# First weights split around the token gather, the last expert's down projection in plain fp32, and two pieces of issue order moved in a one-core transformer layer

## The chip, the cores and the metric

The kernel runs on 1 core of one Trainium2 chip. The metric is device time in microseconds (us) of one execution; lower is better. A run's time lies a little above the span of its trace, which goes from the first to the last instruction.

## The reference

One backbone layer over 1024 latent tokens and 256 context tokens, width 1024: a mixer (latent attention in parallel with a bidirectional mLSTM, merged and projected), then a mixture of 16 SwiGLU experts in which every expert chooses its 128 tokens, then a final RMSNorm. Everything is float32. The part that the change is about, cut:

```python
aff = softmax(x @ w_router)                       # (1024, 16)
g, idx = top_k(aff.T, 128)                        # each expert takes 128 tokens
xs = x[idx]                                       # gathered tokens, per expert
a = xs @ w_e_gate[e]; u = xs @ w_e_up[e]          # 1024 x 1024 each
y = (silu(a) * u) @ w_e_down[e] * g[e]            # 1024 x 1024
out = rmsnorm(x + g2 * scatter_add(idx, y), final_norm)
```

Attention: `p = softmax(q k^T * scale)`, `o = p v`, 8 heads, 1024 queries by 1280 keys.

## The kernel before

Nearly every matmul is done in three fp32r products. A float32 operand is cut into `hi` (ScalarE, a cast to fp32r, an ACT CAST in the rows) and `lo = raw - hi` (VectorE, a DVE TENSOR_TENSOR); the product is hi·hi + hi·lo + lo·hi. The class `Weights` (L769 on) brings the expert weights in blocks of 128x2048 (1 MB each, 12 per expert: 8 for the gate and up projection, 4 for the down projection, index `j`), on the queue of SyncE (SP), 14 raw buffers ahead. `Weights.split` (L862) makes `hi` (L879) and `lo` (L880) of a block; there are three buffers of each (`N_HI`). Instructions are ordered by a planner: it takes those that it thinks ready, by the order in which the program names them; `tc.high_priority()` puts a stretch ahead, and `tc.issue_after(x)` keeps what is in it behind `x` on `x`'s engine.

**Routing and the first tokens.** `Merge.rest` (L1056) ends with the last tile's router and the sort that finds each expert's threshold; it calls `W.split(1)` (L1167), so block 0 is cut there. `moe` (L1178) builds a mask from the threshold, calls `W.split(2)` behind the count of the mask (L1234), sums the mask by matmuls into `pre`, and makes `taken` (L1245), which stands behind the low part of block 1, and `slot` (L1247). `mark(e)` (L1250) writes a one-hot matrix of the expert's tokens: on VectorE for expert 0 (L1256), by eight GpSimd (POOL) instructions for the others (L1254). `pick(e)` (L1259) turns it into token numbers by eight small matmuls and gathers the tokens with an indirect DMA that GpSimd issues (L1278). Behind the matmuls of `pick(0)` eleven matmuls with no use for their result keep TensorE busy. `turn_x(e, q)` (L1292) transposes half of the gathered tokens on TensorE (L1299), scales and shifts them out of PSUM (L1307; for expert 0 half of them on VectorE, L1305) and cuts them into `xh`, `xl` (L1183, L1184).

**The expert loop** (L1341). For expert `e`, two half passes of four blocks each (`products`, L1311) fill `pa` and `pu`; `act` (L1327) makes silu(pa)·pu; `turn` (L1283) transposes that and cuts it into `hd`, high by ScalarE (L1289) and low by VectorE (L1290). Then four blocks of the down projection fill `py`. Between them stand, in this order: `turn` of the second half behind block 0, `pick(e + 2)` and `turn_x(e + 1, 0)` behind block 1, `turn_x(e + 1, 1)` behind block 2. All of them write transposes or sums into one PSUM name, `tr`, which has two buffers. At the end VectorE scales `py` into `y` (L1371), and GpSimd adds it into `acc_d` in HBM by an indirect DMA (L1372).

**The last expert** (L1377 to L1440). Its own 128 rows are gathered back from `acc_d` (L1378), and all 1024 rows are loaded from `acc_d` (L1388) as eight tiles. The last four weight blocks are cut like the others and kept whole (L1406), the down projection runs as 48 fp32r matmuls, column half after column half (L1408 to L1416), and only then come the eight tiles' norm: squares on ScalarE (L1397), an inverse root of about a dozen small VectorE instructions (`rstd_dve`, L143), and the scaling by VectorE (L1400) with a store for each tile. The expert's own rows are put together in `z` (L1421, L1422), normed with them (L1423) and written last, by an indirect DMA that waits for all eight stores (L1436).

**Attention** (L1443 on) works in 32 groups of 256 queries. `scores(g)` ends with the running maximum halved (L1554); behind it stands `low(g - 1, 0)`, the low part of one block of the previous group's exponentials (L1619). `peak(g)` transposes the maxima (L1563) and reduces them to `mq` (L1566), with `low(g - 1, 1)` behind it; `peak2(g)` spreads `mq` by two more transposes (L1573).

Of the kernel before, what the change touches and what calls it, by code (L numbers as in the profile page):

```python
# [23 lines left out]
F32 = mybir.dt.float32  # L24
# [9 lines left out]
P = 128  # L34
# [734 lines left out]
class Weights:  # L769
# [92 lines left out]
    def split(self, upto, engine=None):  # L862
        while self.cut < min(upto, 12 * NE):
# [3 lines left out]
            if not 12 * NE - 4 <= j < 12 * NE - 2:  # L867
                hi, lo = self.halves()
            else:
                hi, lo = [self.buffer(2 * j - 12 * NE + 6 + x, F32R) for x in range(2)]  # L870
            self.parts[j] = hi, lo
# [10 lines left out]
            if self.cut == upto:  # L882
                return done
# [90 lines left out]
class Merge:  # L974
# [81 lines left out]
    def rest(self, aff, thr, pool):  # L1056
# [110 lines left out]
        W.split(1)  # L1167
# [10 lines left out]
def moe(tc, A, out, aff, thr, W, h2_d, acc_d, ident, bcols, rstd, dump):  # L1178
    nc = tc.nc
    V, S, G, TE = nc.vector, nc.scalar, nc.gpsimd, nc.tensor  # L1180

    def split(hi, lo, raw):
        S.copy(hi, raw)  # L1183
        V.tensor_sub(lo, raw, hi)  # L1184
# [4 lines left out]
    with ExitStack() as st:  # L1189
# [43 lines left out]
        with tc.issue_after(counted.ins):  # L1233
            done = W.split(2)  # L1234
# [24 lines left out]
        def pick(e):  # L1259
# [23 lines left out]
        def turn(src, hi, lo, q):  # L1283
# [5 lines left out]
            S.copy(hi[:, 4 * q:4 * q + 4, :], t3)  # L1289
            V.tensor_sub(lo[:, 4 * q:4 * q + 4, :], t3, hi[:, 4 * q:4 * q + 4, :])  # L1290

        def turn_x(e, q):  # L1292
# [4 lines left out]
            for c in range(4):  # L1297
                k = 4 * q + c
                TE.transpose(tr[:, c * P:(c + 1) * P], xg[e][:, k * P:(k + 1) * P], ident)  # L1299
# [9 lines left out]
            split(hi, lo, t)  # L1309
# [16 lines left out]

        def act(pa, pu):  # L1327
# [6 lines left out]
        picked, got, W.after = pick(0)  # L1334
        for q in range(2):
            turn_x(0, q)
# [4 lines left out]
        for e in range(NE):  # L1341
            j = 12 * e
            hd = []
            hs = []
# [12 lines left out]
            if e + 1 < NE:  # L1357
                for q in range(4):
# [18 lines left out]
            rows = p7.tile([P, D], F32, name="xg", bufs=2)  # L1377
            G.indirect_dma_start(out=rows, out_offset=None, in_=acc_d,  # L1378
                                 in_offset=bass.IndirectOffsetOnAxis(ap=idx[e][:, :1], axis=0))
            fn = p7.tile([P, D], F32, name="y", bufs=1)  # L1380
            nc.sync.dma_start(fn, rows_bcast(A["final_norm"], D))
            junk = W.narrow().bitcast(BF16)
            xs, stores = [], []
            for m in range(4):
                x = W.buffer(12 * NE + 2 + m)
                for a in range(2):
                    i = 2 * m + a
                    nc.sync.dma_start(x[:, a], acc_d[i * P:(i + 1) * P])  # L1388
                xs += [x[:, 0], x[:, 1]]
            ss = p7.tile([P, 10], F32, name="fss")  # L1390
# [680 lines left out]
```

## Time and profile before

| | |
|---|---|
| time, median of 3 runs | 2005.15 us (2004.23 to 2007.27) |
| the profiled execution: its own time, its span | 2006.65 us, 2004.9 us |
| mean granted TensorE clock | 0.983 |
| TensorE (PE) busy | 1906.5 us, 95% of the span |
| VectorE (DVE), ScalarE (ACT), GpSimd (POOL) busy | 1397.4 us, 1060.5 us, 554.3 us |
| moved by DMA | 384.77 MB, mean 192 GB/s |

Times in rows are microseconds from the span's start, or the length of an instruction. A row of the timeline has the start, the length, the engine, the line, the operation, what it writes and reads, and in brackets the idle time of the engine before it with what ended it. PE rows of length 0.39 overlap: matmuls are pipelined, so their pace is read from start to start. Plain fp32 matmuls appear as two records each, fp32r ones as one.

### The profile page before, as it was taken

Reading aid. Unit: us, or ns where it says so; the run is one execution under the profiler, and the core shown is the slowest. Engines: PE = TensorE matmul, PEld = TensorE weight load, DVE = VectorE, ACT = ScalarE, POOL = GpSimd, SP = SyncE. Lnnn points to the kernel's source line nnn. Section 1 sums busy time; section 2 is a strip of 40 time slices with the busy share of each in tenths; the row PEclk is TensorE's granted clock in tenths of the full one; section 3 lists DMA queues with packets and bytes.
Section 4 is the critical chain, followed back from the end, with each engine's and each line's share of the span. In section 5 each row is a group of like instructions: output and inputs, shape, how many; then the busy total and the mean of one; then the engine's idle time right before and its main releaser. Section 6 shows DMA issues by size and latency. Waiting matters only on the chain. (4 is left out here: it accounts for less than half of the span.)

```text
span 2004.9 us, 28234 instructions
## 1 busy us (share of the span) xinstructions
PE 1906.5 (95%) x10454; PEld 1607.3 (80%) x10454; DVE 1397.4 (70%) x2492; ACT 1060.5 (53%) x1611; POOL 554.3 (28%) x491
## 2 busy tenths in 40 slices
PE   7999999999999999899999999996999999999994
PEld 3898888888877878789999898884787878878873
DVE  6454555112367788676777768667899999999897
ACT  5554421212336686534334344332778778787774
POOL 0000000000034022165544445001445646455400
PEclk9999999999999999999999999997999999999997
DMA  7153376223069060311311111547799999999984
GB/s 307 55 148 99 117 241 217 88 84 110 32 234 327 6 218 30 93 56 56 102 51 51 49 48 44 210 153 274 270 372 387 382 380 388 383 385 381 377 285 185
DMA packets 156746, 384.77 MB, mean 192 GB/s; under 512 B 10160, under 2 KB 94720, under 8 KB 138432
## 3 DMA queue, kind: packets, MB, share of 16 engines
q1 hardware_dynamic: 141552, 328.68, 45.6%
q0 software_dynamic: 12752, 45.90, 7.4%
q10 hardware_dynamic: 2304, 8.39, 1.0%
q8 instruction: 82, 1.34, 0.3%
q14 instruction: 56, 0.46, 0.1%
HBM read 326.00 MB, written 56.93 MB: 191 GB/s over the span
## 5 line engine op out<-in xcount | busy, mean ns | idle before, releaser
L85 PE MATMUL mm<-hT,whi 128*128 128x512 f32 (+1 forms) x1392 | 415.0, 381 | 2.6 <-DVE hT L304 2.3
L85 PEld LDWEIGHTS mm<-hT,whi 128*128 128x128 f32 x1392 | 255.1, 189 | 51.9 <-DVE hT L304 2.4
L85 PE MATMUL mm<-hT,wlo 128*128 128x512 f32 (+1 forms) x696 | 262.9, 378 | 0.3 <-DVE wlo L89 0.3
L880 DVE TENSOR_TENSOR lo<-raw_l,hi 128x2048 fp32r<-128x2048 f32 x92 | 210.8, 2298 | 21.9 <-ACT hi L879 19.6
L1254 POOL TENSOR_SCALAR g<-iota,slot 128x128 bf16<-128x128 f32 x120 | 206.5, 1733 | 0.0
L879 ACT CAST hi<-raw_l 128x2048 fp32r<-128x2048 f32 x92 | 176.1, 1916 | 34.6 <-PE pu L1187 25.8
L1187 PE MATMUL py<-hi,hd 128*128 128x512 f32 x496 | 168.3, 401 | 0.0
L85 PEld LDWEIGHTS mm<-hT,wlo 128*128 128x128 f32 x696 | 131.3, 189 | 24.6 <-DVE wlo L89 0.7
L89 DVE TENSOR_TENSOR wlo<-wraw,whi 128x1024 fp32r<-128x1024 f32 x38 | 46.5, 1223 | 140.9 <-ACT whi L88 140.9
L880 DVE TENSOR_TENSOR lo<-xca,hi 128x2048 fp32r<-128x2048 f32 x54 | 123.6, 2297 | 17.5 <-ACT hi L879 16.5
L1610 POOL TENSOR_TENSOR es<-es,e 128x512 f32<-128x512 f32 x96 | 124.8, 1300 | 7.0
L1604 ACT ACTIVATE e<-s 128x512 f32<-128x512 f32 x160 | 94.4, 611 | 48.7 <-PE s L1450 48.7
L879 ACT CAST hi<-xca 128x2048 fp32r<-128x2048 f32 x54 | 102.9, 1907 | 25.5 <-PE pu L1187 19.7
L1610 POOL TENSOR_TENSOR es<-e 128x512 f32<-128x512 f32 x32 | 41.7, 1302 | 263.7 <-ACT e L1604 263.7
L88 ACT CAST whi<-wraw 128x1024 fp32r<-128x1024 f32 x38 | 40.0, 1051 | 128.2 <-PE mm L85 124.4
L1550 DVE TENSOR_TENSOR mx<-mx,s 128x512 f32<-128x512 f32 x128 | 87.8, 686 | 27.2 <-PE s L1450 24.6
L1278 POOL DMA_INDIRECT xg<-h_d,idx x16 | 35.8, 2235 | 255.9 <-PE tr L1299 238.2
L1187 PEld LDWEIGHTS py<-hi,hd 128*128 128x128 f32 x496 | 92.1, 188 | 17.7 <-ACT hd L1289 0.2
L1187 PE MATMUL pa<-lo,xh 128*128 128x512 f32 x256 | 100.3, 392 | 3.4 <-DVE lo L880 3.4
L1187 PE MATMUL pa<-hi,xh 128*128 128x512 f32 x256 | 101.4, 396 | 0.3 <-ACT xh L1183 0.3
L1578 ACT CAST qm<-sm 64x256 fp32r<-64x256 f32 x32 | 11.8, 367 | 167.8 <-PE sm L1573 167.8
L1187 PE MATMUL pu<-hi,xl 128*128 128x512 f32 x256 | 100.3, 392 | 0.0
(499 smaller groups left out, 4998.0 us busy)
## 6 DMA issues: line engine op xcount, KB each, us to landing
raw_l<-in_wgu SPq DMA_DIRECT2D x60, 1024.0 KB
xca<-in_wgu SPq DMA_DIRECT2D x37, 1024.0 KB
raw_l<-in_wd SPq DMA_DIRECT2D x32, 1024.0 KB
ha<-in_wgu SPq DMA_DIRECT2D x20, 1024.0 KB
wraw<-in_win SPq DMA_DIRECT2D x38, 512.0 KB
xca<-in_wd SPq DMA_DIRECT2D x19, 1024.0 KB
wt<-in_wmod_b SPq DMA_DIRECT2D x32, 512.0 KB
vk_d<-vk SPq DMA_DIRECT2D x16, 640.0 KB
```

The costliest lines, as they stand in the source:

```text
L85: return TE.matmul(o, l, r, start=start, stop=stop, skip_group_check=True)
L88: S.copy(hi, raw)
L89: V.tensor_sub(lo, raw, hi)
L879: self.nc.scalar.copy(h, w)
L880: done = (engine or self.nc.vector).tensor_sub(l, w, h)
L1187: return TE.matmul(o, l, r, start=start, stop=stop, skip_group_check=True)
L1254: G.tensor_scalar(oh[:, o, :], iota, slot[:, o, e:e + 1], None, op0=ALU.is_equal)
L1278: got = G.indirect_dma_start(out=xg[e], out_offset=None, in_=h2_d, in_offset=bass.IndirectOffsetOnAxis(ap=idx[e][:, :1], axis=0))
L1550: V.tensor_max(new if p > 1 else new.rearrange("p (a b) -> p a b", a=2), old, ps if p > 1 else ps.rearrange("p (a b) -> p a b", a=2))
L1578: S.copy(qm[64:], row[64:])
L1604: S.activation(E[p], ps, AF.Exp)
L1610: G.tensor_add(s, E[0] if p == 1 else s, E[p])
```

## The change

The diff, cut to its core:

```diff
 class Weights:
-    def split(self, upto, engine=None):
-        while self.cut < min(upto, 12 * NE):
+    def split(self, upto, later=None):
+        while self.cut < min(upto, 12 * NE - 4):
...
             for h, l, w in views:
                 self.nc.scalar.copy(h, w)
-                done = (engine or self.nc.vector).tensor_sub(l, w, h)
+                if later is None:
+                    self.nc.vector.tensor_sub(l, w, h)
+                else:
+                    later.append(lambda h=h, l=l, w=w: self.nc.vector.tensor_sub(l, w, h))
 class Merge, rest:
-        W.split(1)
+        W.lows = []
+        W.split(1, W.lows)
 def moe:
         with tc.issue_after(counted.ins):
-            done = W.split(2)
+            W.split(N_HI, W.lows)
...
-        with tc.issue_after(done.ins):
-            V.scalar_tensor_tensor(taken, pre, 1.0, mk, op0=ALU.add, op1=ALU.mult)
+        V.scalar_tensor_tensor(taken, pre, 1.0, mk, op0=ALU.add, op1=ALU.mult)
...
+        def warm(after, n):
+            with tc.issue_after(after.ins):
+                ps = ps7.tile([P, 512], F32, name="pu", bufs=2)
+                for x in range(n):
+                    mm(ps, W.parts[0][0][:, 0, :P], W.parts[0][0][:, 0, :512], True, True)
   pick:
             if e == 0:
-                with tc.issue_after(done.ins):
-                    ps = ps7.tile([P, 512], F32, name="pu", bufs=2)
-                    for x in range(11):
-                        mm(ps, W.parts[0][0][:, 0, :P], W.parts[0][0][:, 0, :512], True, True)
+                warm(done, 16)
   turn:
             S.copy(hi[:, 4 * q:4 * q + 4, :], t3)
+            if hi.dtype == F32:
+                return
   turn_x:
+            if e == 0 and q == 1:
+                warm(turned, 7)
...
         mark(0)
         picked, got, W.after = pick(0)
+        with tc.issue_after(picked.ins):
+            for f in W.lows[:2]:
+                f()
         for q in range(2):
-            turn_x(0, q)
+            done = turn_x(0, q)
+        with tc.issue_after(done.ins):
+            W.lows[2]()
...
         for e in range(NE):
+            if e == NE - 1:
+                others()
...
-                        t = W.wide_hi(F32R)
+                        t = W.wide_hi(F32R if e + 1 < NE else F32)
...
+                    if e == NE - 1 and hf == 1 and q == 2:
+                        squares(0, 2)
...
             if e + 1 < NE:
+                turn_x(e + 1, 0)
                 for q in range(4):
                     products(j + 8 + q, py, hd, q == 0, q == 3)
                     if q == 0:
                         turn(hs[1], *hd, 1)
-                    if q == 1 and e + 2 < NE:
+                    if q == 1:
+                        turn_x(e + 1, 1)
+                    if q == 2 and e + 2 < NE:
                         pick(e + 2)
-                    if q in (1, 2):
-                        turn_x(e + 1, q - 1)
...
-            W.split(12 * NE)
+            turn(hs[1], *hd, 1)
+            squares(2, 8)
+            scale(0, 2)
+            scale(2, 5)
+            scale(5, 8)
             for o in range(2):
                 for k in range(8):
-                    mm(py[o], hd[0][:, k, :], wh, k == 0, False)
-                    mm(py[o], hd[0][:, k, :], wl, False, False)
-                    mm(py[o], hd[1][:, k, :], wh, False, k == 7)
+                    mm(py[o], hd[0][:, k, :], w[:, k % 2, c], k == 0, k == 7)
+                with tc.high_priority():
+                    V.scalar_tensor_tensor(z[:, c], py[o], gat[e], g2row[:, c], op0=ALU.mult, op1=ALU.mult)
+                    V.tensor_add(z[:, c], z[:, c], rows[0][:, c])
+                    S.activation(junk[:, :512], z[:, c], AF.Square, accum_out=zs[:, o:o + 1])
+            with tc.high_priority():
+                V.tensor_add(zs[:, 0:1], zs[:, 0:1], zs[:, 1:2])
+                rstd(p7, zs[:, 2:3], zs[:, 0:1], D)
+                V.scalar_tensor_tensor(z, z, zs[:, 2:3], fn[0], op0=ALU.mult, op1=ALU.mult)
+                own = G.indirect_dma_start(out=out, out_offset=bass.IndirectOffsetOnAxis(ap=idx[e][:, :1], axis=0),
+                                           in_=z, in_offset=None)
 attention:
             MX[g] = pk.tile([P, 256], F32, name="mm", bufs=2)
-            halved = V.tensor_max(MX[g], mx[:, :256], mx[:, 256:])
-            with tc.issue_after(halved.ins):
-                low(g - 1, 0)
+            V.tensor_max(MX[g], mx[:, :256], mx[:, 256:])
...
             with tc.issue_after(found.ins):
-                low(g - 1, PARTS[1])
+                for p in PARTS[:2]:
+                    low(g - 1, p)
```

In the last expert's new loop `w` is the raw float32 block. `others()` is new and holds what stood at the head of the last expert's tail: the gather of its own rows, the load of the final norm's weights and the eight loads from `acc_d`, now into the raw buffers of blocks that are four places earlier in the rotation. `squares(a, b)` squares tiles a to b; `scale(a, b)` makes their inverse roots at once, scales them and stores each; `zs` holds the sums of `z` alone.

## Rows read from the trace of the kernel before

**Rows 1.** The page, busy time of each engine over the span

```profile
PE 1906.5 (95%) x10454; PEld 1607.3 (80%) x10454; DVE 1397.4 (70%) x2492; ACT 1060.5 (53%) x1611; POOL 554.3 (28%) x491
```

**Rows 2.** Who waited for whom, TensorE: us in total, times, longest

```profile
PE tr L1299 <- DVE hd L1290: 6.7, 13, 0.5
...
PE sm L1573 <- DVE mq L1566: 3.9, 21, 0.5
...
PE pa L1187 <- DVE lo L880: 3.4, 2, 1.7
```

**Rows 3.** Timeline from the last expert's loads to the end: start, length, engine, line

```profile
1951.55 1.91 SPq L1388 DMA_DIRECT2D raw_l<-acc_d  x4
...
1966.66 4.02 PE L1187 MATMUL py<-raw_l,hd 128*128 128x512 f32 x17
...
1978.09 0.39 PE L1187 MATMUL py<-hi,hd 128*128 128x512 f32 x1
...
1979.56 0.69 DVE L1422 TENSOR_TENSOR xg<-xg 128x512 f32<-128x512 f32 x1
...
1988.88 0.16 DVE L162 TENSOR_SCALAR rv<-fss 128x5 f32<-128x5 f32 x1
...
1991.08 4.87 DVE L1400 SCALAR_TENSOR_TENSOR ha<-ha,frs,y 128x1024 f32<-128x1024 f32 x4
...
1999.88 0.99 POOL L1436 DMA_INDIRECT out_dram<-xg,idx  x1 [47.16 <-DMA out_dram<-ha]
```

**Rows 4.** Timeline of TensorE in the mLSTM, plain fp32 matmuls of 512 columns

```profile
642.72 1.88 PE L1732 MATMUL mm<-xca,fold 128*128 128x512 f32 x4
644.44 1.99 PE L1732 MATMUL st<-qT,xca 128*128 128x128 f32 x16
```

**Rows 5.** Timeline at an expert boundary (experts 13 and 14), ScalarE

```profile
1897.08 1.91 ACT L879 CAST hi<-raw_l 128x2048 fp32r<-128x2048 f32 x1
1900.10 1.51 ACT L1307 ACTIVATE g<-tr,bcols 128x128 f32<-128x128 f32 x4 [1.11 <-PE tr L1299]
...
1903.28 0.64 ACT L1183 CAST xh<-g 128x512 fp32r<-128x512 f32 x1
```

**Rows 6.** Timeline of the routing, VectorE and TensorE

```profile
1382.85 2.27 DVE L880 TENSOR_TENSOR lo<-ha,hi 128x2048 fp32r<-128x2048 f32 x1
1382.94 0.37 PE L950 MATMUL so<-sc,ident 64*16 64x64 f32 x2 [5.14 <-DVE sc L944]
...
1390.52 0.27 PE L1187 MATMUL tr<-above,cst 128*128 128x128 bf16 x1
1391.88 0.41 DVE L1245 SCALAR_TENSOR_TENSOR g<-tr,mk 128x256 f32<-128x256 f32 x1
1392.21 2.28 DVE L880 TENSOR_TENSOR lo<-raw_e,hi 128x2048 fp32r<-128x2048 f32 x1
1394.41 0.28 DVE L1247 SCALAR_TENSOR_TENSOR slot<-g 128x128 f32<-128x128 f32 x1
```

**Rows 7.** Timeline: first gather, tokens' transposes; a later gather and low part

```profile
1397.63 1.07 POOL L1278 DMA_INDIRECT xg<-h_d,idx  x1 [17.49 <-DVE gt L1275]
...
1402.20 1.06 PE L1299 MATMUL tr<-ident,xg 128*128 128x128 f32 x8 [1.39 <-DMA xg<-h_d,idx]
...
1438.07 2.29 DVE L880 TENSOR_TENSOR lo<-raw_l,hi 128x2048 fp32r<-128x2048 f32 x1
...
1438.79 2.39 POOL L1278 DMA_INDIRECT xg<-h_d,idx  x1 [29.02 <-PE tr L1299]
```

**Rows 8.** One line's instructions, L1254: ns min/median/max, first and last start

```profile
L1254 POOL TENSOR_SCALAR g<-iota,slot x120: 590/704/4514, 1398.8 to 1881.0; 128x128 bf16<-128x128 f32 x120
```

**Rows 9.** Busy time by stretch: length, PE, PEld, DVE, ACT, POOL, granted clock, DMA

```profile
1408.00:1410.00 2.00, 2.00 (x6) 1.59 (x5) 0.00 (x0) 0.00 (x0) 1.61 (x3) 0.50 0.04 8
```

**Rows 10.** Timeline of one attention group, VectorE

```profile
1101.68 1.22 DVE L1619 TENSOR_TENSOR tl<-e,th 128x512 fp32r<-128x512 f32 x1
...
1102.83 0.41 DVE L1566 TENSOR_REDUCE mq<-sm 128x2 f32<-128x256 f32 x1
```

More of the change, by code (lines that the diff above doesn't have):

```diff
@@ L866, in split @@
             raw = self.raw[j]
[L867 to L871, printed above, removed]
+            hi, lo = self.parts[j] = self.halves()
             if j == ONCE[1]:
@@ L1308, in turn_x @@
             hi, lo = [x[:, 4 * q:4 * q + 4, :].rearrange("p a b -> p (a b)") for x in xsT[e]]
-            split(hi, lo, t)
+            S.copy(hi, t)
+            return V.tensor_sub(lo, t, hi)
         def products(j, ps, l, start, stop):
@@ L1325, in products, with others, squares, scale @@
                     mm(ps[o], ll, wh[:, slice(o * 512, o * 512 + 512)], False, stop and c == 1)
+        rows, fn, xs, stores = [], [], [], []
+        def others():
+            rows.append(p7.tile([P, D], F32, name="xg", bufs=2))
+            G.indirect_dma_start(out=rows[0], out_offset=None, in_=acc_d,
+                                 in_offset=bass.IndirectOffsetOnAxis(ap=idx[NE - 1][:, :1], axis=0))
+            fn.append(p7.tile([P, D], F32, name="y", bufs=1))
+            nc.sync.dma_start(fn[0], rows_bcast(A["final_norm"], D))
+            for m in range(4):
+                x = W.buffer(12 * NE - 2 + m)
+                for a in range(2):
+                    i = 2 * m + a
+                    nc.sync.dma_start(x[:, a], acc_d[i * P:(i + 1) * P])
+                xs.extend([x[:, 0], x[:, 1]])
+        def squares(a, b):
+            for i in range(a, b):
+                S.activation(junk, xs[i], AF.Square, accum_out=ss[:, i:i + 1])
+        def scale(a, b):
+            rstd(p7, rs[:, a:b], ss[:, a:b], D)
+            for i in range(a, b):
+                V.scalar_tensor_tensor(xs[i], xs[i], rs[:, i:i + 1], fn[0], op0=ALU.mult, op1=ALU.mult)
+                stores.append(nc.sync.dma_start(out[i * P:(i + 1) * P], xs[i]))
         def act(pa, pu):
@@ L1343, in moe @@
             hd = []
+            if e == NE - 1:
+                others()
+                junk = W.narrow().bitcast(BF16)
+                ss, rs, zs = [p7.tile([P, 8], F32, name=x) for x in ("fss", "frs", "fzs")]
             hs = []
@@ L1374, in moe @@
                 continue
[L1377 to L1390, printed above, removed]
-            rs = p7.tile([P, 10], F32, name="frs")
-            def alike(t, x):
-                return t if len(x.shape) == 2 else t.rearrange("p (c d) -> p c d", d=256)
-            def squares(k, x):
-                S.activation(alike(junk, x), x, AF.Square, accum_out=ss[:, k:k + 1])
-            def scale(k, x):
-                return V.scalar_tensor_tensor(x, x, rs[:, k:k + 1], alike(fn, x), op0=ALU.mult, op1=ALU.mult)
-            def write(i):
-                scale(i, xs[i])
-                stores.append(nc.sync.dma_start(out[i * P:(i + 1) * P], xs[i]))
-            W.split(12 * NE)
+            turn(hs[1], *hd, 1)
[3 more added lines that the diff above has]
+            scale(5, 8)
             z = p7.tile([P, D], F32, name="xg", bufs=2)
@@ L1410, in moe @@
                 for k in range(8):
-                    wh, wl = [w[:, k % 2, c] for w in W.parts[j + 8 + k // 2]]
-                    mm(py[o], hd[0][:, k, :], wh, k == 0, False)
-                    mm(py[o], hd[0][:, k, :], wl, False, False)
-                    mm(py[o], hd[1][:, k, :], wh, False, k == 7)
-                    if o == 0 and k == 1:
-                        turn(hs[1], *hd, 1)
-            squares(0, xs[0])
-            squares(1, xs[1])
-            for o in range(2):
-                c = slice(o * 512, o * 512 + 512)
-                V.scalar_tensor_tensor(z[:, c], py[o], gat[e], g2row[:, c], op0=ALU.mult, op1=ALU.mult)
-                V.tensor_add(z[:, c], z[:, c], rows[:, c])
@@ L1423, in moe @@
-            S.activation(junk, z, AF.Square, accum_out=ss[:, 8:9])
-            rstd(p7, rs[:, 0:2], ss[:, 0:2], D)
-            for i in range(2, 8):
-                squares(i, xs[i])
-            write(0)
-            write(1)
-            rstd(p7, rs[:, 2:4], ss[:, 2:4], D)
-            write(2)
-            write(3)
-            rstd(p7, rs[:, 4:9], ss[:, 4:9], D)
-            for i in (4, 5, 6, 7):
-                write(i)
-            scale(8, z)
-            own = G.indirect_dma_start(out=out, out_offset=bass.IndirectOffsetOnAxis(ap=idx[e][:, :1], axis=0),
-                                       in_=z, in_offset=None)
+                    w = W.raw[j + 8 + k // 2]
@@ new lines, in moe @@
+                    if len(w.shape) == 4:
+                        mm(py[o].rearrange("p (c d) -> p c d", d=256), hd[0][:, k, :], w[:, k % 2, 2 * o:2 * o + 2, :],
+                           k == 0, k == 7)
+                    else:
+                        mm(py[o], hd[0][:, k, :], w[:, k % 2, c], k == 0, k == 7)
[3 more added lines that the diff above has]
+                    S.activation(junk[:, :512], z[:, c], AF.Square, accum_out=zs[:, o:o + 1])
```

7 lines of the change are left out of this document (1 added, 6 removed).

## Prediction

> **What bounds the kernel now.** The page comes first: TensorE is busy for 95% of the span [rows 1], so a change gains only where TensorE stands still or has nothing left. Second, the waits of TensorE, added up by who ended them [rows 2]. Three of them belong to this change: 6.7 us before the transposes of gathered tokens (13 times 0.5), 3.9 us before the transposes of `mq`, and 3.4 us before the low part of a weight block (2 times 1.7). Third, the timeline of the end [rows 3]: the last down projection starts at 1966.66, its last matmul ends at 1978.09 + 0.39 = 1978.5, and the span ends at 2004.9. TensorE does nothing for the last 26.4 us; VectorE norms eight other tiles one after another there. Fourth, the routing [rows 6] and the first gather [rows 7], where TensorE also waits for VectorE.
>
> All sums are made against the profiled execution, 2006.65 us, of which 2004.9 are the span; the median of the runs is 1.5 us less.
>
> **1. The tail.** Call 1966.66 zero; the end now is at 38.2. *Added on TensorE:* a plain fp32 matmul of 512 columns takes 0.86 (two of them between 642.72 and 644.44 [rows 4]). Sixteen take 13.8. The fp32r ones come at 0.227 (17 within 4.02, the last 0.39 of it its own length [rows 3]); the 48 removed took 10.9. So TensorE pays 2.9. With about 0.5 for the four transposes of `hs[1]` (eight take 1.06 [rows 7]) its end moves from 11.8 to 14.3; only the first half of `hd` is needed for the first matmuls, which covers the silu, product and transposes of the second. *Removed:* the last four cuts, 1.91 of ScalarE [rows 5] and 2.3 of VectorE each [rows 6], and the norm of the others behind the matmuls. *Moved:* eight scalings (4.87 for four) and three inverse roots (2.2 each, 1988.88 to 1991.08) are 16.3 of VectorE [rows 3]. VectorE is free of cuts some 2.5 before zero, and the first tiles are loaded by then: the loads start at 1951.55, 15 before zero, when expert 14's rows are in HBM; naming them earlier cannot start them earlier. On SP's queue they stand behind all weight loads, already issued, and only the stores stand behind them. So the others are done near 14 to 15.5, their stores 3.9 later (1995.95, the last scaling's end, to 1999.88 [rows 3]), under the chain of `z`. *That chain,* from 14.3: hand-over 0.3, two steps of 0.69 [rows 3], a half row's square 0.64 (as long as the 128x512 cast [rows 5]) with 0.2 to read the sum, nine small steps of 0.2 (eleven in 2.2), scaling 1.22, 1.2 to GpSimd (an estimate between nothing and the 3.9 above), and 5.0 from the write's issue to the end (1999.88 to 2004.9): 26.1. I add 0.6 for half a scaling that VectorE may be in. **38.2 - 26.7 = 11.5 gained.** Bounds: 13.5 if every hand-over is free, 8 if two or three scalings fall behind `z`.
>
> **2. Expert boundaries.** `turn_x(e + 1, 0)` no longer follows `pick` and the turn of `hs[1]` on the two `tr` buffers: between two uses of one buffer there are now two blocks of twelve matmuls, 24 x 0.227 = 5.4. The 6.7 of [rows 2] can go, and the 3.4 with it, if ScalarE keeps up. Late next is ScalarE: 1.51 + 0.64 for the first half of the tokens [rows 5] now stand in front of the cast for a block that TensorE wants 6.75 after the up projection's end (two blocks, two sets of transposes at 0.53, one 0.227). Silu (0.64, as a cast of its shape), 2.15, the cast 1.91 and the low part 2.28 end at 6.98. So 0.2 late there, and about as much again where the second half meets the next expert's block 0. I take 0.35 at each of 15 boundaries, 5.1, nearer to that sum than to the 1.7 of [rows 2]. **10.1 - 5.1 = 5 gained.** Bounds: 10.1 gained (nothing late), 5 lost (1.0 each). The gather of expert `e + 2` goes one block later, 2.7; it has most of an expert's time as cover, and without that cover it would cost the 2.7.
>
> **3. Routing and first tokens.** Three low parts leave VectorE's chain. The first holds the sort from 1383.31 (the matmul's end) to about 1385.05, 1.6 with a hand-over; the second holds `taken` from 1390.79 to 1391.88, 0.95; the third stands between `taken`, done at 1392.29, and `slot` at 1394.41, 2.1 [rows 6]. Together 4.65. The casts of blocks 1 and 2 go to ScalarE where it waits; cost 0, and their cover is that wait. But two low parts, 4.56, now follow `pick(0)` on VectorE at once, and GpSimd issues the gather beside them. With VectorE idle that takes 1.07; beside a low part (1438.07 to 1440.36) it took 2.39, to 0.82 behind that part's end [rows 7]. A GpSimd instruction of 0.59 took up to 4.51 [rows 8], as long as two low parts. VectorE starts them at about 1397.06 of the old time, so the issue ends at 1397.06 + 4.56 + 0.82 = 1402.4 instead of 1398.70: 3.75 given back, and the tokens, which now come 3.5 behind the issue [rows 7], with it. Behind the gather on GpSimd stands `mark(1)`, eight times 0.59; it still ends before the first tokens are cut, so the matmuls of `pick(1)` don't hold TensorE. The third low part follows the cut of the tokens and is wanted two blocks later; hidden. The 16 and 7 filler matmuls run where TensorE waits; before, the clock was at 0.50, its lower level, as late as 1408 to 1410 [rows 9], in the first products. If they keep it at the upper level, that returns at most 1.6 (8 matmuls at 0.43 instead of 0.23); a longer wait can as well lengthen the low stretch, up to all 24 matmuls of two blocks, 4.8. I take 0 for it. **About 1 gained.** Bounds: 6.2 gained (gather free, clock kept), 3.9 lost.
>
> The Trainium skill, "SBUF — State Buffer", section "SBUF: two separate sides", says that a VectorE operation with two SBUF inputs and a GpSimd operation that reads SBUF take the shared ports in turn, each for a whole instruction. By that the gather would pass between the two low parts, and the sum would be 22.8 gained, 1982.3 (a part of rival (a)); by the rows it is 20.5. [rows 8] has a GpSimd instruction that did not pass.
>
> **4. Attention.** `low(g - 1, 0)`, 1.22 in the group shown, stood between the maximum and `mq` [rows 10]; behind `mq` it can't hold it. The 3.9 of [rows 2] go. Two low parts in a row then stand in front of the subtraction that `peak2` ends with; VectorE has idle time there, and I allow 0.9 for groups in which it has not. **3 gained.** Bounds: 3.9 gained, 0.5 lost.
>
> **Sum:** 11.5 + 5 + 1 + 3 = 20.5 gained; 2006.65 - 20.5 = 1986.1 in a profiled execution, **1984.6** against the median of 2005.15.
>
> **Rivals.** (a) *The gather is not held, or only by one low part.* For it: small VectorE steps could leave it a gap; against it: [rows 8]. By one low part (2.28 less) 1982.3; free, with the clock kept, 1979.4. Chance 0.2. (b) *The boundaries lose.* For it: ScalarE has 12 casts and the tokens' 4.3 beside 144 matmuls, 33 us, and [rows 2] has 1.7 twice where the order fell so. At 1.0 late each, the lower bound of part 2, 1994.6; halfway, 1989.6. Chance 0.18. (c) *Slower.* Same place: if the planner puts the whole 2.15 in front of two casts that have no room, TensorE waits about 2.15 at each of 15 boundaries, 32.3 against 10.1 gained; 22.2 lost and 15.5 from the other parts give 2011.9. It decides from (10.1 + 15.5) / 15 = 1.7 a boundary, as long as the longest wait now. Against it: the parts of a block have three buffers each, and a wait once taken gives time to what follows. Chance 0.05. (d) *The tail does not overlap.* If squares or scalings are ordered behind `z` after all, the old 26.4 stay and the 2.9 come on top: 11.5 turn into -2.9, 1999.0. Against it: `z` has high priority. Chance 0.04. My forecast has the rest, 0.53.
>
> **The range** runs from 1975, between the free gather and all boundaries kept (1974.3), to 1993, most of the way to the lower bound of part 2; outside it lie (c), (d), the end of (b) and a part of (a) with full gains, together 2 in 10. About 0.2% (4 us) is what a measurement of this kernel can tell from no change. Faster by more than that: forecast, (a), (b), (d) and a little of (c), 0.93; within it 0.03; slower 0.04.
>
> **What would show it.** Right: plain `py` matmuls at 0.86 for some 14 us and an end about 12 behind the last of them; no wait of the tokens' transposes for `hd`; `mq` gone from TensorE's waits; `slot` right behind `taken`; the first gather's issue over 4 us long. Wrong: a gather of about 1 us (part 3 too small), new waits for `lo` or `xh` at expert starts (part 2 too large), stores of the others behind `z` (part 1 too large).

## Result and profile after

The changed kernel takes 1991.68 us (median of 4 runs, 1989.38 to 1992.14) against 2004.69 (4 runs, 2003.54 to 2007.27) beside it: a ratio of 0.9931, 95% interval 0.9918 to 0.9943, or 13.0 us. The forecast was 1984.6, 20.5 gained; the result lies in its range. Its profiled execution takes 1992.02, of which 1990.2 are the span, 14.7 less than before. TensorE's share hardly changes; VectorE and ScalarE each lose a little. The page, busy time of each engine (as [rows 1]):

```profile
PE 1907.9 (96%) x10450; PEld 1604.2 (81%) x10450; DVE 1378.2 (69%) x2495; ACT 1053.5 (53%) x1609; POOL 537.7 (27%) x491
```

Who waited for whom, TensorE, of the changed kernel (us in total, times, longest; as [rows 2]):

```profile
PE pa L1182 <- ACT hi L876: 8.1, 13, 0.6
...
PE s L1645 <- DVE kl L1459: 2.5, 8, 0.6
...
PE pv L1455 <- DVE tl L1623: 1.5, 3, 0.5
```

The transposes' wait for `hd` (6.7) is gone, and so is nearly all of the waits for low parts (3.4, now 0.5) and for `mq` (3.9, now 0.5). In their place stands a new one, 13 times 0.6, of an expert's first product for a cast.

To see where the time went, the span is cut at marks that TensorE's rows give in both kernels: attention's first and last product, the first matmul of the first pick, the first product of expert 0, the last product of the last up projection, the end. Each number is the distance of two starts, from one profiled execution of each kernel.

| stretch | before | after | change | forecast |
|---|---|---|---|---|
| start to attention (untouched) | 823.0 | 820.6 | -2.4 | 0 |
| attention | 430.9 | 425.1 | -5.8 | -3 |
| attention's end to the first pick | 141.5 | 137.6 | -3.9 | -4.65 |
| first pick to first product | 9.9 | 11.5 | +1.6 | +3.75 |
| experts, to the last up projection's end | 561.0 | 562.6 | +1.6 | -5 |
| tail | 38.4 | 32.8 | -5.7 | -11.5 |

The first row is code that the change does not touch: so far do two executions differ there. No term came out as forecast. Four readings, one for each part:

**Tail.** Timeline of the end of the changed kernel (as [rows 3]): start, length, engine, line.

```profile
1960.14 0.17 DVE L162 TENSOR_SCALAR rv<-fss 128x2 f32<-128x2 f32 x1 [1.09 <-ACT g L1348]
...
1962.31 2.48 DVE L1353 SCALAR_TENSOR_TENSOR raw_l<-raw_l,frs,y 128x1024 f32<-128x1024 f32 x2
...
1963.71 0.60 PE L1285 MATMUL tr<-ident,g 128*128 128x128 f32 x4
1964.34 0.58 ACT L1287 COPY hd<-tr 128x512 f32<-128x512 f32 x1 [2.44 <-PE tr L1285]
1964.82 1.06 ACT L1348 ACTIVATE g<-raw_l 128x1024 bf16<-128x1024 f32 x1
1967.19 0.17 DVE L162 TENSOR_SCALAR rv<-fss 128x3 f32<-128x3 f32 x1 [2.40 <-ACT g L1348]
...
1970.23 1.88 PE L1182 MATMUL py<-raw_l,hd 128*128 128x512 f32 x4
1971.75 1.28 DVE L1353 SCALAR_TENSOR_TENSOR raw_l<-raw_l,frs,y 128x1024 f32<-128x1024 f32 x1
1972.94 0.75 DVE L1434 SCALAR_TENSOR_TENSOR xg<-py,gt,g2row 128x512 f32<-128x512 f32 x1
1973.61 1.28 DVE L1353 SCALAR_TENSOR_TENSOR raw_l<-raw_l,frs,y 128x1024 f32<-128x1024 f32 x1
1974.80 0.69 DVE L1435 TENSOR_TENSOR xg<-xg 128x512 f32<-128x512 f32 x1
...
1980.29 1.28 DVE L1353 SCALAR_TENSOR_TENSOR raw_l<-raw_l,frs,y 128x1024 f32<-128x1024 f32 x1
1981.48 1.28 DVE L1440 SCALAR_TENSOR_TENSOR xg<-xg,fzs,y 128x1024 f32<-128x1024 f32 x1
1985.24 0.99 POOL L1441 DMA_INDIRECT out_dram<-xg,idx  x1 [32.74 <-DMA out_dram<-raw_l]
```

Zero is 1957.86 here, the end of the last up projection. TensorE ends at 1972.1, 14.25 behind it, as forecast. But on VectorE the scalings of the others still run: the last one ends at 1981.57, 23.7 behind zero, and `z` is scaled only at 1982.76. Two idle stretches answer to each other: ScalarE sits 2.44 in front of the copy of `hd`, whose transposes TensorE does only behind eight down matmuls; the squares stand behind that copy; and VectorE sits 2.40 for them. Then `z`'s own write waits for the others' stores: it is issued at 1985.24, 2.5 behind `z`, where it comes 0.3 behind `z` in the two kernels with nothing else to wait for (e7 and e11 below).

**Attention.** Timeline of TensorE at the maximum of one group, kernel before:

```profile
1008.57 1.03 PE L1450 MATMUL pv<-e,vf 128*128 128x256 f32 x4
1009.76 0.43 PE L1573 MATMUL sm<-ident,mq 128*128 128x128 f32 x2 [0.17 <-DVE mq L1566]
```

The same place in the changed kernel:

```profile
1005.80 1.03 PE L1455 MATMUL pv<-e,vf 128*128 128x256 f32 x4
1006.67 0.38 PE L1577 MATMUL sm<-ident,mq 128*128 128x128 f32 x2
```

From the four matmuls' start to the transposes' it takes 1.19 before and 0.87 after: 0.32 gained, where the list of waits has 0.17. A wait there is counted from the modelled end of the matmul in front, which lies behind the moment at which the next one could have started. Over the 29 groups where a matmul of `e` stands directly in front, that pair of starts goes from 0.473 to 0.216 in the mean, 7.5 us in all. About 2 come back as other waits: 1.5 for `tl`, and 2.5 for `kl`, which had 1.8 before.

**Routing.** Timeline of VectorE, GpSimd and TensorE in the changed kernel (as [rows 6, 7]):

```profile
1384.82 4.48 DVE L880 TENSOR_TENSOR lo<-ha,hi 128x2048 fp32r<-128x2048 f32 x2
...
1385.46 2.60 POOL L1276 DMA_INDIRECT xg<-h_d,idx  x1 [12.66 <-DVE gt L1273]
...
1391.62 1.06 PE L1299 MATMUL tr<-ident,xg 128*128 128x128 f32 x8 [0.79 <-DMA xg<-h_d,idx]
...
1394.88 0.50 PE L1182 MATMUL pa<-hi,xh 128*128 128x512 f32 x1 [0.31 <-ACT xh L1311]
```

The stretch behind its first product (columns as in [rows 9]):

```profile
1396.00:1398.00 2.00, 2.00 (x11) 1.64 (x10) 2.00 (x2) 0.06 (x1) 2.00 (x2) 1.00 0.03 8
```

The gather's issue ends at 1388.06, 1.0 behind the end of the first low part (half of 4.48) and ahead of the second's. It was held by one, not by both. The granted clock behind the first product is 1.00, the upper level of 2.4 GHz; before it was at 0.50 there.

**Boundaries.** Timeline of one boundary of the changed kernel, TensorE, ScalarE and VectorE:

```profile
1820.93 0.40 PE L1182 MATMUL py<-lo,hd 128*128 128x512 f32 x1
1821.95 0.49 PE L1182 MATMUL pa<-hi,xh 128*128 128x512 f32 x1 [0.63 <-ACT hi L876]
1822.28 0.40 PE L1182 MATMUL pu<-hi,xh 128*128 128x512 f32 x1
1822.57 0.73 PE L1182 MATMUL py<-hi,hd 128*128 128x512 f32 x2
...
1819.38 0.61 ACT L1287 CAST hd<-tr 128x512 fp32r<-128x512 f32 x1
1819.99 1.91 ACT L876 CAST hi<-raw_e 128x2048 fp32r<-128x2048 f32 x1
...
1815.01 0.68 DVE L1359 TENSOR_TENSOR g<-pu,g 128x512 f32<-128x512 f32 x1
...
1819.02 2.29 DVE L878 TENSOR_TENSOR lo<-ha,hi 128x2048 fp32r<-128x2048 f32 x1 [0.90 <-ACT hi L876]
1821.23 0.68 DVE L1312 TENSOR_TENSOR xl<-g,xh 128x512 fp32r<-128x512 f32 x1
1821.83 0.68 DVE L1290 TENSOR_TENSOR hd<-tr,hd 128x512 fp32r<-128x512 f32 x1
```

VectorE at one boundary of the kernel before:

```profile
1858.82 0.68 DVE L1330 TENSOR_TENSOR g<-pu,g 128x512 f32<-128x512 f32 x1
...
1864.26 0.68 DVE L1290 TENSOR_TENSOR hd<-tr,hd 128x512 fp32r<-128x512 f32 x1
```

Two products of the next expert stand in the middle of the down projection, and the first waits for its cast. An expert takes 36.0 from first product to first product, 12 times, where before it took 35.6. (The first product stands early at 13 boundaries: expert 0 seems to take 31.1 by it, and expert 13 40.1.)

### The profile page after: what moved, and what is told of

It reads as the page before. It is cut to its first block, busy times and chain, and to the rows that moved or that the text cites. A ratio compares the mean times of both kernels' runs of the same rounds, so it can differ in the third digit from the quotient of the medians.

```text
span 1990.2 us, 28210 instructions
## 1 busy us (share of the span) xinstructions
PE 1907.9 (96%) x10450; PEld 1604.2 (81%) x10450; DVE 1378.2 (69%) x2495; ACT 1053.5 (53%) x1609; POOL 537.7 (27%) x491
## 4 chain that ended last, share of the span: by engine, by line
PE 79%; DVE 9%; ACT 6%; issue 3%; DMA 2%; SPq 0%; POOLq 0%; POOL 0%; DVEq 0%; ACTq 0%
PE mm L85 24%; PE s L1455 11%; PE pa L1182 8%; PE pu L1182 8%; PE py L1182 4%; PE mm L985 4%; PE pv L1455 4%; PE ab L1736 3%; ACT hi L876 3%; PE c L1736 2%; PE tr L85 2%; DVE tl L1623 2%; ACT g L1309 1%; PE tp L85 1%; DVE lo L878 1%
## 5 line engine op out<-in xcount | busy, mean ns | idle before, releaser
L1255 POOL TENSOR_SCALAR g<-iota,slot 128x128 bf16<-128x128 f32 x120 | 174.9, 1472 | 244.7 <-PE tr L1285 244.7
L1182 PE MATMUL pu<-hi,xh 128*128 128x512 f32 x256 | 99.8, 390 | 0.0
L1182 PE MATMUL pu<-lo,xh 128*128 128x512 f32 x256 | 99.8, 390 | 0.0
```

The lines of the kernel that those rows point to most:

```text
L1182: return TE.matmul(o, l, r, start=start, stop=stop, skip_group_check=True)
L1255: G.tensor_scalar(oh[:, o, :], iota, slot[:, o, e:e + 1], None, op0=ALU.is_equal)
```

## Experiments

Each kernel was timed beside the kernel before, whose medians were 2005.0 to 2006.4; the changed kernel's ratio to compare with is 0.9931 (0.9918 to 0.9943). An interval is 2 to 3 us wide to each side, so effects of a few us are told apart by the stretches of the profiled executions, cut as above. Code that no edit touches shows what these are worth: attention starts between 819.0 and 823.6 in the fourteen kernels, and takes 425.1 to 427.8 in the twelve with its new order. From the first pick on, stretches of unchanged code repeat better: the first product within 0.5, the experts within 1.1, the tail within 0.05.

| kernel | ratio | attention | first pick to first product | experts | tail |
|---|---|---|---|---|---|
| before | 1 | 430.9 | 9.9 | 561.0 | 38.4 |
| changed | 0.9931 | 425.1 | 11.5 | 562.6 | 32.8 |
| e1 boundary as before | 0.9925 | 427.8 | 11.4 | 559.6 | 32.8 |
| e2 attention as before | 0.9967 | 431.7 | 11.6 | 563.1 | 32.8 |
| e3 tail as before | 0.9957 | 426.7 | 11.6 | 562.0 | 38.5 |
| e4 gather first | 0.9949 | 425.4 | 11.9 | 565.4 | 32.8 |
| e5 products in order | 0.9979 | 426.1 | 11.5 | 568.5 | 36.3 |
| e6 fillers as before | 0.9945 | 427.1 | 12.0 | 564.1 | 32.8 |
| e7 turn early | 0.9932 | 425.4 | 11.8 | 562.7 | 29.9 |
| e8 two scalings off VectorE | 0.9934 | 425.8 | 11.5 | 562.7 | 30.7 |
| e9 product turned first | 0.9905 | 425.7 | 11.5 | 555.1 | 32.8 |
| e10 pick later | 0.9950 | 425.6 | 12.0 | 564.8 | 32.8 |
| e11 both turns first | 0.9892 | 427.2 | 11.3 | 555.2 | 29.9 |
| e12 one root less | 0.9882 | 425.2 | 11.5 | 555.3 | 28.7 |

### e1: the boundary as before

```diff
             if e + 1 < NE:
-                turn_x(e + 1, 0)
...
-                    if q == 1:
-                        turn_x(e + 1, 1)
-                    if q == 2 and e + 2 < NE:
+                    if q == 1 and e + 2 < NE:
                         pick(e + 2)
+                    if q in (1, 2):
+                        turn_x(e + 1, q - 1)
```

> The changed kernel with the order at the experts' boundaries as before. Theory (boundaries cost time in the changed kernel: an expert takes 36.00 there and 35.60 before, its first product waits 0.6 for a cast): 13 boundaries give 0.4 each back, 5.2, less the 3.4 of waits for low parts that may return: 2 to 5 us faster than the changed kernel, 1987 to 1990, with 35.6 an expert. Rival, the forecast (5 gained by the new order): 5 us slower, 1997, with over 36.2 an expert.

Measured: ratio 0.9925 (0.9912 to 0.9939); an expert takes 35.6 again, the waits of [rows 2] for `hd` (6.7, 13 times) and for low parts (3.3) are back, and still the experts' stretch is 3.0 shorter than in the changed kernel. So the new order lost 3.0, and the forecast's sign there was wrong. The total moved by less than its interval; the stretch decides. This kernel also prices the clock alone: its first expert takes 35.94 against 37.93 before, in the same order of work, 2.0, all of it in that expert's first 48 products (11.0 against 13.0).

### e2: attention as before

```diff
-            V.tensor_max(MX[g], mx[:, :256], mx[:, 256:])
+            halved = V.tensor_max(MX[g], mx[:, :256], mx[:, 256:])
+            with tc.issue_after(halved.ins):
+                low(g - 1, 0)
...
-                for p in PARTS[:2]:
-                    low(g - 1, p)
+                low(g - 1, PARTS[1])
```

> The changed kernel with attention's low parts where they were before. Theory (the wait for mq cost 7.5 from start to start, twice what the list of waits has, and 2 of it came back as waits for low parts): 5.5 us slower than the changed kernel, 1997.2, all of it between attention's first and last matmul. Rival, the forecast: 3 us slower, 1994.7.

Measured: ratio 0.9967 (0.9957 to 0.9978), 7.2 us slower than the changed kernel by the ratios. Attention takes 431.7, against 425.1 to 427.8 (mean 426.1) in the twelve with the new order: 5.6. The theory holds.

### e3: the tail as before

The edit puts back the four cuts and the old code behind the last up projection as the diff shows them removed.

> The changed kernel with the tail as before: split matmuls, and the other tokens' norm behind them. Theory (the tail gained what the two traces show from the last up projection's end to the end of the span, 38.05 against 32.38): 5.7 us slower than the changed kernel, 1997.4. Rival, the forecast: 11.5 us slower, 2003.2. Second rival: the changed tail also shortens the last expert before that point (four cuts less); then 7 to 8 us slower.

Measured: ratio 0.9957 (0.9944 to 0.9971), 5.2 us slower; the tail 38.5 against 32.8, the experts 562.0 against 562.6. The theory holds: the tail is worth 5.7, and nothing beyond the 1.1 of scatter lies ahead of the last up projection's end.

### e4 and e10: the gather in front of the low parts

```diff
             for f in W.lows[:2]:
-                f()
+                tc.add_manual_dep(f().ins, W.after.ins.name,
+                                  mybir.DependencyInfo(mybir.DependencyClass.Sync, mybir.DependencyReason.DATA),
+                                  reason="the gather goes first")
```

e10 has this edit, and `pick(1)` stands in the program behind the first expert's third block.

> The changed kernel with the first two low parts behind the first gather's issue, by a semaphore. Theory (the gather stood behind one low part, 2.60 instead of 1.07, and the tokens come a fixed 3.5 behind its issue): the gather's issue takes 1.1, the first product starts 1.5 earlier, 1.5 us faster than the changed kernel, 1990.2. Rival: the low parts now end 1.7 later and hold the cut of the tokens; then the first product starts less than 0.5 earlier and the time is the same.

> The run with the gather first, and besides the second pick's matmuls stand behind the first expert's third block. Theory (in that run the pick's matmuls waited 2.5 for GpSimd's marks and held the first product, and the clock fell in that wait): the first product comes 10.0 to 10.4 behind the first pick instead of 11.5, at 0.23 a product, 1.2 us faster than the changed kernel. Rival: TensorE stands still 1 us between the fillers and the first product, and the clock falls anyway: first products at 0.43, 1 us slower.

Measured, e4: ratio 0.9949 (0.9935 to 0.9962), 3.6 slower. Timeline of GpSimd and TensorE in e4:

```profile
1385.92 1.08 POOL L1276 DMA_INDIRECT xg<-h_d,idx  x1 [12.32 <-DVE gt L1273]
...
1390.18 1.06 PE L1299 MATMUL tr<-ident,xg 128*128 128x128 f32 x8
...
1395.72 0.19 PE L1182 MATMUL tr<-aux,g 128*128 128x5 bf16 x1 [0.39 <-POOL g L1255]
1395.77 0.78 PE L1182 MATMUL pa<-hi,xh 128*128 128x512 f32 x1
1396.34 0.63 PE L1182 MATMUL pa<-lo,xh 128*128 128x512 f32 x1
```

The first half of the theory holds: the issue takes 1.08, and the tokens come 6.35 behind the first pick instead of 8.24. The gain is lost one step later, in neither of the two ways expected: the second pick's matmuls, in front of the first product in TensorE's order, wait for GpSimd's marks until 1395.72. The marks are late because the two low parts, moved behind the gather, now stand beside them. VectorE's low parts in e4, and GpSimd's marks that begin by 1393 (ns, shortest, median, longest; as [rows 8]):

```profile
1387.15 4.66 DVE L880 TENSOR_TENSOR lo<-ha,hi 128x2048 fp32r<-128x2048 f32 x2 [1.79 <-POOL ax L1279]
...
L1255 POOL TENSOR_SCALAR g<-iota,slot x4: 591/614/4510, 1387.1 to 1392.8; 128x128 bf16<-128x128 f32 x4
```

The second mark, begun inside the first low part, ends only 0.4 behind the second: 4.51 instead of 0.59. TensorE stands still in parts of that wait, and then 13 products run at 0.43, the lower level of 1.2 GHz: the first product comes 0.4 later and the experts take 2.8 more.

e10 was to take that pick away, but the planner left TensorE's order as in e4: its first product again comes 12.0 behind the first pick, behind the same matmuls, its second mark takes 4.52, and ratio (0.9950, 0.9936 to 0.9963) and stretches repeat e4. What the freed gather is worth with the pick out of the way stays untried.

### e6: the fillers as before

`warm(done, 16)` becomes `warm(done, 11)`, and the 7 behind the tokens' transposes go.

> The changed kernel with 11 filler matmuls behind the first pick and none behind the tokens' transposes, as before. Theory (the fillers kept the clock; in the kernel before, the first products ran at a granted clock of 0.50): about 10 products at 0.43 instead of 0.23, granted clock 0.5 in the 2 us behind the first product, 2 us slower, 1994. Rival, the forecast's zero: first products at 0.23 as well, same time.

Measured: ratio 0.9945 (0.9931 to 0.9958), 2.8 us slower; the first product 0.5 later, the experts 1.5 longer, 2.0 together. Its first expert takes 32.6, where it takes 31.1 to 31.3 in the changed kernel, e2, e3, e7 and e8; the first seven products are the slow ones. Busy time by stretch in e6 (columns as above):

```profile
1394.00:1396.00 2.00, 0.36 (x8) 0.27 (x7) 1.35 (x5) 1.81 (x5) 2.00 (x4) 0.50 0.99 418
1396.00:1398.00 2.00, 1.99 (x5) 1.60 (x6) 2.00 (x4) 0.55 (x1) 2.00 (x3) 0.50 0.11 45
```

TensorE works 0.36 of the 2 us ahead of the first product, and the granted clock is at 0.50. The fillers are worth 2.0, not zero.

### e5: the next expert's products behind the down projection

```diff
-                    products(j + 4 * hf + q, ps, xsT[e], q == 0, q == 3)
+                    with tc.issue_after(down.ins) if e > 0 and hf == 0 and q == 0 else nullcontext():
+                        products(j + 4 * hf + q, ps, xsT[e], q == 0, q == 3)
...
-                    products(j + 8 + q, py, hd, q == 0, q == 3)
+                    down = products(j + 8 + q, py, hd, q == 0, q == 3)
```

> The changed kernel, in which the next expert's first products may not be placed ahead of the last down matmul. Theory (the loss at the boundaries comes from two products of the next expert that stand five blocks of work early in TensorE's order and wait 0.6 for a cast that nobody wants so early; the moved transposes themselves are good): the wait goes, no wait for hd comes back, an expert takes 34.9 to 35.2 instead of 36.0, 10 to 14 us faster than the changed kernel, 1978 to 1982. Rival, the forecast's own reason (ScalarE is late because of the tokens' 2.15): the wait moves to the new place of the first products, an expert takes 35.6 or more, at most 5 faster, 1987 or more.

Measured: ratio 0.9979 (0.997 to 0.9988), 9.6 us slower than the changed kernel; an expert takes 36.45. Both theories fall: there is no wait for a weight block at all. Who waited for whom, TensorE, e5:

```profile
PE py L1182 <- DVE hd L1290: 18.8, 15, 1.3
```

So the two early products did no harm; they filled a hole. What is late is the second half of `hd`, wanted by the third down block: in the changed kernel's rows above the down products that stand behind the two early ones start at 1822.57, just behind the end of `hd`'s low part. That low part ends at 1822.51, 7.5 behind the start of the product that it is made from (1815.01); before, the same way took 6.1 (1858.82 to 1864.94). Its cast stands behind the tokens' scaling and a block's cast on ScalarE, its low part behind a block's low part and the tokens' `xl` on VectorE. A block's cast and low part stood in front of them in the kernel before, too; the tokens' scaling, `xh` and `xl` are the work that the change moved there. (The tail loses 3.5 besides: the two down matmuls that had stood early now add to the block in front of the transposes of `hs[1]`, the squares come 0.8 later still, and three scalings fall behind `z`'s.)

### e9: the product turned first at every boundary

```diff
                     if q == 0:
-                        turn(hs[1], *hd, 1)
+                        with tc.high_priority():
+                            turn(hs[1], *hd, 1)
```

> The changed kernel, in which the turn of the last half of the product (transposes, cast, low part) has high priority at every boundary. Theory, new after the run with the products in order (the third down block waits for hd's low part, because the tokens' scaling, a block's cast and low part and the tokens' own casts now stand in front of it on ScalarE and VectorE): hd comes 1.5 to 2 earlier, no wait for it is left, an expert takes 34.9 to 35.4, 8 to 14 us faster than the changed kernel, 1978 to 1984. Rival (ScalarE and VectorE have no room, whatever the order): the wait moves to a weight block's hi or lo, an expert takes 35.6 or more, at most 5 faster.

Measured: ratio 0.9905 (0.9892 to 0.9919), 5.2 us faster than the changed kernel by the ratios; the first eleven experts take 34.9 to 35.2, most of them 35.05, and the experts' stretch is 7.5 shorter. `hd` at one boundary of e9, timeline of VectorE and ScalarE:

```profile
1663.12 0.68 DVE L1359 TENSOR_TENSOR g<-pu,g 128x512 f32<-128x512 f32 x1
...
1664.85 0.60 ACT L1287 CAST hd<-tr 128x512 fp32r<-128x512 f32 x1
...
1666.16 0.68 DVE L1290 TENSOR_TENSOR hd<-tr,hd 128x512 fp32r<-128x512 f32 x1
```

What the list of TensorE's waits has left for the experts of e9 ahead of the last down projection, but for 0.3 in front of the very first product:

```profile
PE pa L1182 <- DVE lo L878: 3.3, 9, 0.6
```

From the product to `hd`'s low part it takes 3.7 now, and nobody waits for it. The theory that e5 gave holds for the first eleven experts. The next four, up to the last expert, take 35.9 to 36.6, with waits for low parts; that is the rival's place, and why it is there only at the end was not followed up. So the expected 8 to 14 became 7.5.

### e7, e8: the tail's squares and VectorE's load

e7 puts the transposes of `hs[1]` behind the second down matmul in TensorE's order; e8 has that, one root for tiles 2 to 7, and two tiles off VectorE:

```diff
-            turn(hs[1], *hd, 1)
             squares(2, 8)
...
+                    if o == 0 and k == 1:
+                        with tc.issue_after(last.ins):
+                            turned = turn(hs[1], *hd, 1)
```

```diff
+                if i in (3, 5):
+                    S.activation(xs[i], xs[i], AF.Identity, scale=rs[:, i:i + 1])
+                    G.tensor_mul(xs[i], xs[i], fn[0])
+                else:
+                    V.scalar_tensor_tensor(xs[i], xs[i], rs[:, i:i + 1], fn[0], op0=ALU.mult, op1=ALU.mult)
```

> The changed kernel, in which the transposes of the last half of the product stand behind two down matmuls in TensorE's order, so that ScalarE's squares don't stand behind them. Theory (the tail is bound by VectorE, which has 22 us of scalings, roots and z's steps from 1960.1 on): squares end 3 us earlier, the end moves by less than 1. Rival (the squares were the cause): the end comes 2.5 to 3.5 earlier, 1988.5.

> As the run with the early turn, and besides one inverse root for tiles 2 to 7 instead of two, and tiles 3 and 5 scaled by ScalarE (by the root) and GpSimd (by the norm's weights). Theory (VectorE bounds the tail): VectorE loses 2.2 of roots and 2.5 of scalings, the span ends 28.2 behind the last up projection instead of 32.4, 4 to 5 us faster than the changed kernel, 1987. Rival (stores or ScalarE bound it, or GpSimd is slow beside VectorE): less than 1.5 faster.

Measured, e7: tail 29.9, 2.9 shorter; ratio 0.9932 (0.9918 to 0.9945), so the total doesn't show it. Timeline of ScalarE in e7, the copy of `hd` and the last square:

```profile
1961.37 0.56 ACT L1287 COPY hd<-tr 128x512 f32<-128x512 f32 x1
...
1966.55 1.06 ACT L1348 ACTIVATE g<-raw_l 128x1024 bf16<-128x1024 f32 x1
```

The rival is right: the squares' order was 2.9 of the tail. The copy starts 2.5 behind the end of the last up projection instead of 6.5, and nothing is idle on VectorE from its first root to the last add of `z`. In e7 the loads of `acc_d` also start earlier (11.0 ahead of the last up projection's end instead of 6.5); e9 has them 10.9 ahead, and its tail is 32.8, so it is the order and not the loads.

Measured, e8: tail 30.7, longer than in e7; ratio 0.9934 (0.9921 to 0.9948). Timeline of VectorE in e8:

```profile
1970.21 5.76 DVE L1357 SCALAR_TENSOR_TENSOR raw_l<-raw_l,frs,y 128x1024 f32<-128x1024 f32 x3
...
1976.56 2.70 DVE L1357 SCALAR_TENSOR_TENSOR raw_l<-raw_l,frs,y 128x1024 f32<-128x1024 f32 x1
```

And of GpSimd there:

```profile
1971.45 6.72 POOL L1355 TENSOR_TENSOR raw_l<-raw_l,y 128x1024 f32<-128x1024 f32 x2 [22.08 <-ACT raw_l L1354]
```

The first two scalings take 1.28 each, as without GpSimd. The third takes 3.36 and ends 1.1 behind GpSimd's first product (1974.89); the fourth takes 2.70 and ends 1.1 behind the second (1978.17). Each of GpSimd's own two in turn ends 2.2 behind a scaling, so the engines went by turns. VectorE lost 3.5 that way, more than its two tiles' 2.5. e12, with the same root and every tile on VectorE, ends at 28.7, 2.0 earlier. The rival's last clause holds. The Trainium skill, "SBUF — State Buffer", section "SBUF: two separate sides", has a port pair that a VectorE operation with two SBUF inputs and a GpSimd operation that reads SBUF lock for a whole instruction. These rows agree.

### e11, e12: both turns first, and one root less

e11 joins e9 and e7; e12 replaces `scale(2, 5)` and `scale(5, 8)` by `scale(2, 8)`.

> The changed kernel with the product's last half turned first at the boundaries and, in the tail, behind two down matmuls. Theory (the two edits act on different stretches, 7.5 between the first product and the last up projection and 2.9 behind it, and add up): span 1979 to 1981, an expert 35.05, the end 29.9 behind the last up projection; 10 us faster than the changed kernel. Rival (what the boundaries gain is lost to later loads in the tail, which wait for expert 14's rows): the end comes over 31 behind the last up projection, 7 faster at most.

> The run with both turns first, and one inverse root for tiles 2 to 7 instead of two. Theory (VectorE is now busy from the first root to the end of the tail): 2.2 of root less, 1.3 of idle in front of the later root, the end 29.0 behind the last up projection instead of 29.9. Rival (the last write waits for the others' stores): the same or up to 1 later.

Measured: e11 0.9892 (0.9875 to 0.9908), experts 555.2, tail 29.9: the two add up. e12 0.9882 (0.9865 to 0.9898), median 1982.1, tail 28.7, 1.15 shorter again. Timeline of GpSimd in e12, the write of `z`'s rows:

```profile
1977.05 0.99 POOL L1444 DMA_INDIRECT out_dram<-xg,idx  x1 [33.19 <-DVE xg L1443]
```

The view names `z`, but the write comes 0.73 behind `z`, not 0.28 as in e7 and e11. It comes 3.65 behind the end of the others' last scaling, the 3.7 at which it follows that scaling where it waits for the stores (the changed kernel, e1, e2, e4, e6, e9, e10). So the stores seem to hold it by some 0.45 still. e12 is the fastest measured, 23 us ahead of the kernel before and some 10 ahead of the changed one; the intervals of e11 and e12 overlap.

## Why the prediction was right, and its terms were not

The time fell inside the range, faster as forecast, 7.1 above the number. That the sum held is in part luck, for errors of both signs met: the tail and the boundaries gave 13.8 less than their terms, attention, routing and clock about 6 more, by the stretches and the runs. Of the signs named for it, the plain matmuls' pace, the transposes without a wait for `hd`, `mq` and `slot` came true; the end came 18.1 behind the last `py` matmul instead of 12, and the first gather's issue took 2.60, not over 4.

- **Tail: 5.7, not 11.5, below its lower bound of 8.** TensorE's 14.3 and the 5.0 behind the write's issue came as computed. The step that failed is "So the others are done near 14 to 15.5": they were done at 23.7. I put VectorE's 16.3 as one block from 2.5 ahead of zero; its first root began 2.3 behind zero, it then stood 2.4 for the squares (e7), and three scalings fell between `z`'s steps and three more between its root and its scaling. That makes `z` 4.5 late (24.9 against 20.4), and the others' stores hold its write until 2.5 behind it, 1.3 more than the 1.2 that I allowed: 5.8 together. My "15 before zero" for the loads was 6.5, since zero moved and the loads did not; e9 against the changed kernel shows that this cost nothing.
- **Boundaries: 3.0 lost, not 5 gained** (e1), inside the bound of 5 lost: rival (b) in part. "Late next is ScalarE: [...] in front of the cast for a block" named the right engine and the wrong customer. The block's cast was in time (e5 has no wait for it); late was `hd`'s second half, which passes both engines behind the work that I had moved ahead of it (e5 shows the wait, e9 what its end is worth; that this lateness is the whole of the 3.0 is argued from the rows, not tried alone). The working counted what the tokens hold up on the weights' path and not on the product's.
- **Routing: 2.7 gained, and 2.0 by the clock.** The low parts out of the chain gave 3.1 to 5.0 in the thirteen kernels with this part, 4.3 in the mean, near the 4.65. Given back were 1.6 instead of 3.75: the gather passed between the two low parts, rival (a); e4 shows the issue free at 1.08. The rule of the Trainium skill that the forecast set aside (the page and section named at e8) fits this gather. My row of 4.51 [rows 8] was no guide to a gather, but it was one to a mark: in e4 one mark waited for both low parts, 4.51, and did not pass between them. That "the matmuls of `pick(1)` don't hold TensorE" was true only because the gather was late: in e4 they did. The clock's term, taken as 0, is 2.0 (e1, e6), above the bound of 1.6 worked out from eight matmuls.
- **Attention: 5.6 (e2), above the bound of 3.9.** "The 3.9 of [rows 2] go" took the list of waits for the cost. From start to start the wait was 7.5.

## What to carry to other kernels

A wait in the list can understate what it costs on a pipelined engine (3.9 for `mq` here, 7.5 from start to start): take the distance of the two starts, and subtract the pace. When work is moved ahead, follow every other consumer of the engines that it passes, not only the nearest one: here the product's second half, a chain of four short steps over three engines, was what the moved tokens held up, and giving that chain priority was worth more (7.5) than the move had cost (3.0). An engine that is to run "beside" another has to be summed from the moment at which its first input lands to its own end, with its idle stretches.

## What the runs showed of the hardware

A DMA with indices that GpSimd issues is held beside VectorE's low parts, and by no fixed time. One line's instructions in the changed kernel, the scatter of an expert's rows (ns, shortest, median, longest):

```profile
L1413 POOL DMA_INDIRECT acc_d<-y,idx x15: 3002/3018/7823, 1435.0 to 1938.4; - x15
```

Before, the median was 1.62 us. Expert 14's took 7.79 (1938.38 to 1946.17) while VectorE ran low parts nearly back to back, and 3.39 in e7, with the same order at that boundary. It ended 1.5 behind the end of the third low part beside it in the changed kernel (1944.69), and 1.5 behind the end of the first in e7 (1941.24). The gather took 2.60 and ended 1.0 behind one low part; the mark of e4 took 4.51 beside two. So an instruction of GpSimd can be passed by more than one VectorE instruction; which of them it loses to was not settled.

GpSimd was no relief for VectorE in e8, where both read SBUF: the two scalings that met a 128x1024 product of GpSimd's took 3.36 and 2.70 instead of 1.28.
